# A hybrid decoder layer with a mixture of experts: another order of output projection and router, one ring slot and one early request more, another end of the last norm

## The chip, the cores and the metric

The kernel runs on one core of a Trainium2 chip. The metric is the device time of one execution in microseconds (us). A core has TensorE (PE) for matmuls, with its weight loads shown as PEld; VectorE (DVE); ScalarE (ACT); GpSimd (POOL); and SyncE (SP), whose queue issues most of the DMAs here. All engines take their instructions from queues of their own, in order, and wait for each other by semaphores. Matmul results land in the banks of PSUM, everything else lives in SBUF, and weights and inputs come from HBM.

## The reference

One layer over 512 tokens of width 1024. A first half mixes tokens; a second half is a feed-forward part with 32 experts, of which each token uses two.

```python
def hybrid_mixer(x, mem, ...):
    proj = x @ w_in                       # queries, keys, values, gates of three branches
    y_a = moba_attention(...); y_b = stick_breaking_attention(...); y_m = memory_attention(...)
    merged = (gates[:, :, 0] * (y_a @ w_br_moba) + gates[:, :, 1] * (y_b @ w_br_sb)
              + gates[:, :, 2] * (y_m @ w_br_mem))
    return merged @ w_out                 # the output projection

def hierarchical_moe(x, ...):
    g_p, g_idx = lax.top_k(softmax(x @ w_router_group + b_router_group), 1)
    e_logits = x @ w_router_expert + b_router_expert     # 4 groups of 8 experts
    top_l, top_i = lax.top_k(e_in_group, 2)              # two experts of the chosen group
    gate = g_p * softmax(top_l)
    ...                                                  # per expert e, on its tokens:
        h = silu(xb @ w_gate[e]) * (xb @ w_up[e]);  y = h @ w_down[e]
    ...                                                  # sum of gate * y over a token's experts

x = layer_norm(alpha * x + hybrid_mixer(x, mem, ...))
x = layer_norm(alpha * x + hierarchical_moe(x, ...))
```

All is float32. Each expert has 6 MB of weights, so 192 MB are read in one execution.

## The kernel before, in words

Tokens stand in four tiles of 128 (t = 0 to 3), channels in eight blocks of 128. Precision in the first half is kept by splitting each operand into a high and a low part of a shorter float and adding three products (mm3, L122): "woh" and "wol" are the parts of the output weights, "mgh" and "mgl" those of the merged branches.

**The end of the first half.** Attention and gates run as a list of jobs. The output projection of the first four channel blocks is done among them; of the last four blocks it is done behind them, in `project` (L825): for a tile t and a half of the columns (c = 0 or 1) nine matmuls for blocks 4 to 6 and three for block 7, whose merged branch is the last to be ready, into a bank of "dn". DVE adds the bank to x1 with row sums (L835), and `norm` follows for the tile: sums (L599), the square on ACT (L601), the second step (L602), two halves of subtract and scale (L606), a power on POOL (L603), two halves of scale and offset (L610). POOL then stores the tile to the scratch "xdr".

**The router**, per tile: T transposes x1 on PE and ACT copies it to "xt" (L648, L649); L multiplies it by the router's weights (L656), and DVE chooses group and experts from the logits in ten short operations (L661 to L672), the last of which writes "ab", the 0/1 table of the tile's experts; R counts places by small matmuls with "ab" (L679 to L682), and DVE turns the counts into places and these into the 0/1 matrix "sel" of the first pair of experts (L684 to L688, L732, L733); A gathers the tile's tokens of the first pair by matmuls with "sel" (L843). A pair is two experts with 64 places each. The string ORDER says in which order PE takes these steps: "G0" is `project` of tile 0, "G30" and "G31" the two halves of tile 3, "T0", "L0", "R0", "A0" the steps above. PE's order is fixed by it; the order of DVE, ACT, POOL and SP is made by a scheduler when the program is built, and is fixed too when it runs.

**The experts.** For each of 16 pairs: up and gate (`up`, L955, tile "gu"), the product (L964), a transpose ("ht"), down (L982, "dn"), and `combine`, which adds the result to x1 for all tiles by matmuls with the 0/1 matrix "sT" (L800, L801). Weights come in halves of 1 MB: two halves each of gate, up and down for two experts, 12 halves a pair, 192 in all. They land in a ring of RA + RB + RC + RD slots, 9 + 4 + 4 + 1 = 18, in four pools ("ring1" to "ring4"), and two halves more in a buffer "once", which is given up after its use. A slot is filled again when PE has used it. The pools open when their memory is free: ring2 before the projection, with 4 halves loaded early; ring1 when the branches are done; ring3 when the projection has read its weights; "once" and ring4 later in the router. `ahead(n)` asks for the next n halves on SP.

After pair 0 stands a loop (L1158) over experts with more than 64 tokens; with these inputs it runs zero times, but its count comes from a table that DVE makes during pair 0, and all engines meet in a barrier around it. Before it, `ahead(BEFORE)` with BEFORE = 6 asks for six halves; every later half is asked for behind the loop, when a slot comes free.

**The end.** `last_norm` scales and shifts x1 in 8 parts of 128 tokens by 512 columns: `inner` on DVE, then `outer`, which for the parts in BYDVE runs on DVE (L1079) and for the others as a matmul with a diagonal matrix onto a bank that holds the offset already (L1106, L1081), with a copy back by ACT (L1082). Each part is stored by SP in the order of the parts (`ship`, L1055).

Of the kernel before, what the change touches and what calls it, by code (L numbers as in the profile page):

```python
# [11 lines left out]
F32 = mybir.dt.float32  # L12
# [5 lines left out]
ALU = mybir.AluOpType  # L18
# [4 lines left out]
P = 128  # L23
# [10 lines left out]
WB, LOOK = 2, 1  # L34
F_M, F_A, F_B = 3.9, 3.9, 3.9
H = (slice(0, 64), slice(64, 128))
RA, RB, RC, RD = 9, 4, 4, 1
HALF = 2048
MIDP = 0
BEFORE = 6  # L40
CW = 184
BIG = 8192.0
XTB = 2
HTB = 1
BYDVE = ((3, 0), (3, 1))
BANKS = ("ht", "gu", "dn", "cb", "xgp", "cb", "", "")
FIRST = (2, 1)
ORDER = "G0 G1 T0 G2 L0 T1 G30 L1 R0 G31 A0 T2 L2 T3 R1 L3 R2 A1 R3 A2 A3"


@with_exitstack
def layer(ctx, tc, xT, xn, memT, w_qk, w_v, w_mk, w_mv, w_g, w_o, rb, oh, ln, wr, br,
# [69 lines left out]
    def mm3(o, pairs, start=True, stop=True):  # L122
        n = len(pairs)
        for i, (lh, ll, rh, rl) in enumerate(pairs):
            pe.matmul(o, lh, rh, start=start and i == 0, stop=False)  # L125
            pe.matmul(o, ll, rh, start=False, stop=False)  # L126
            pe.matmul(o, lh, rl, start=False, stop=stop and i == n - 1)  # L127
# [459 lines left out]
    def bank3(tag):  # L587
        return ps.tile([P, 512], F32, name=tag, tag=tag, bufs={"gu": 2, "dn": 2, "xgp": 1, "ht": 1, "cb": 2}[tag])
# [232 lines left out]
    pairs[0].start()  # L821
    first = []

    def project(t, cols=(0, 1)):

        ts = slice(t * P, (t + 1) * P)
        os_ = [bank3("dn") for c in cols]
        for ks in (range(3), range(3, 4)):
            for c, o in zip(cols, os_):
                r = slice(c * 512, (c + 1) * 512)  # L830
                mm3(o, [(mg[4 + k][0][:, ts], mg[4 + k][1][:, ts], wo[k][0][:, r], wo[k][1][:, r]) for k in ks],
                    start=ks[0] == 0, stop=ks[0] == 3)
        for c, o in zip(cols, os_):
            r = slice(c * 512, (c + 1) * 512)
            ve.scalar_tensor_tensor(out=x1[:, t, r], in0=x1[:, t, r], scalar=1.0, in1=o, op0=ALU.mult, op1=ALU.add,  # L835
                                    accum_out=sm[:, t, c:c + 1])
        if 1 in cols:
            norm(t, sm, lnb, op)
            gp.dma_start(xdr[ts, :], x1[:, t, :])
# [10 lines left out]
    with tc.manual_schedule(engines={mybir.EngineType.PE}):  # L850
        xt_ = {}
        for step in ORDER.split():
            t = int(step[1])
            if step[0] == "G":
                project(t, (0, 1) if len(step) == 2 else (int(step[2]),))
                if t == 0:
                    first += [bank3("xgp"), bank3("cb")]
            elif step[0] == "T":
                xt_[t] = turn_x(t)
            elif step[0] == "L":  # L860
                route(t, xt_[t])
            elif step[0] == "R":
                place(t)
            else:
                gather0(t)
        settle()
# [179 lines left out]
    def last_norm(gb):  # L1046

        col = lambda i: slice(i * 512, (i + 1) * 512)

        def inner(t, i):  # L1050
            x = x1[:, t, col(i)]
            ve.scalar_tensor_tensor(out=x, in0=x, scalar=sm2[:, t, 5:6], in1=gb[:, 0, col(i)], op0=ALU.add, op1=ALU.mult)  # L1052

        def ship(t, i):
            nc.sync.dma_start(out[t * P:(t + 1) * P, col(i)], x1[:, t, col(i)])  # L1055

        m, d = sm2[:, :, 5], sm2[:, :, 6]
        ve.tensor_tensor(out=m, in0=sm2[:, :, 0], in1=sm2[:, :, 1], op=ALU.add)
        ve.tensor_scalar(out=m, in0=m, scalar1=-1.0 / D, scalar2=None, op0=ALU.mult)
        ve.scalar_tensor_tensor(out=d, in0=sm2[:, :, 0], scalar=2.0 / D, in1=m, op0=ALU.mult, op1=ALU.add)  # L1060
        ve.tensor_tensor(out=d, in0=d, in1=d, op=ALU.mult)
        inner(0, 0)

        v = [sm2[:, :, i] for i in range(8)]
        ve.scalar_tensor_tensor(out=v[3], in0=v[3], scalar=EPS * D ** 3 / 4.0, in1=v[4], op0=ALU.add, op1=ALU.add)
        ve.scalar_tensor_tensor(out=v[3], in0=v[3], scalar=4.0 / D ** 3, in1=v[6], op0=ALU.mult, op1=ALU.subtract)
        gp.tensor_tensor(out=v[7], in0=v[3], in1=half.to_broadcast([P, TT]), op=ALU.pow)
        inner(0, 1)
        inner(1, 0)
        diag = late[0].tile([P, TT, P], F32, name="diag", tag="hT", bufs=1)  # L1070

        def spread(ts):
            ve.tensor_tensor(out=diag[:, ts, :], in0=ident.unsqueeze(1).to_broadcast([P, ts.stop - ts.start, P]),
                             in1=v[7][:, ts].unsqueeze(2).to_broadcast([P, ts.stop - ts.start, P]), op=ALU.mult)

        def outer(t, i):
            x = x1[:, t, col(i)]
            if (t, i) in BYDVE:
                ve.scalar_tensor_tensor(out=x, in0=x, scalar=v[7][:, t:t + 1], in1=gb[:, 1, col(i)], op0=ALU.mult, op1=ALU.add)  # L1079
            else:  # L1080
                pe.matmul(os_[t, i], diag[:, t, :], x, start=False, stop=True)  # L1081
                sc.copy(x, os_[t, i])  # L1082
            ship(t, i)

        inner(1, 1)
        spread(slice(0, 2))
        for t in range(2):
            outer(t, 0)
            outer(t, 1)
        inner(2, 0)  # L1090
        spread(slice(2, 4))
        outer(2, 0)
        inner(2, 1)
        outer(2, 1)
        inner(3, 0)
        inner(3, 1)
        outer(3, 0)
        outer(3, 1)

    os_ = {}  # L1100

# [6 lines left out]
    def last(hT):  # L1108
        pair = pairs[15]
        b = [None, None]  # L1110

        def part(c, ks):
            if ks[0] == 0:
                pair.room(c)
                b[c] = bank3("dn")
                held[:] = [weights(30 + q, 2, c) for q in range(2)]
            for k in ks:
                for q in range(2):
                    pe.matmul(b[c][H[q]], hT[:, k, H[q]], held[q][:, k * 512:(k + 1) * 512], start=k == 0, stop=k == 3)  # L1119

        part(0, range(4))
        pair.out = b[0]
        pair.finish(0)
        part(1, range(2))
        lnt = ring().rearrange("p (a b) -> p a b", b=D)
        for i in range(2):
            nc.sync.dma_start(lnt[:, i, :], ln[2 + i:3 + i, :].to_broadcast([P, D]))
        last_sums(0, ("cb", "xgp", "gu", "cb"))
        part(1, range(2, 4))
        ve.tensor_copy(pair.y_h[1], b[1])  # L1130
        ve.tensor_tensor(out=pair.y_l[1], in0=b[1], in1=pair.y_h[1].bitcast(F32), op=ALU.subtract)
        offset(lnt, 0, 2)
        last_sums(1, ("cb", "xgp", "gu", "cb"))
        offset(lnt, 2, 6)
        last_norm(lnt)

    hTs = []
# [20 lines left out]
    with tc.For_i(0, nov, 1) as i:  # L1158
# [13 lines left out]
        ve.tensor_copy(pair.si[0:64, 0:1], sp[0:64, 0:1])  # L1172
        ve.tensor_copy(pair.si[0:64, 2:3], sp[0:64, 1:2])
        pair.rows(64)
        pair.xg = late[0].tile([P, KT, 64], F32, name="xg_o")
        o = bank3("xgp")
        for k in range(KT):
            pe.transpose(o[:, k * 64:(k + 1) * 64], xrow[0][0:64, k * P:(k + 1) * P], ident[0:64, 0:64])
# [120 lines left out]
```

## Time and profile before

| | us |
|---|---|
| three runs | 942.25, 937.72, 940.51 (median 940.51) |
| the profiled execution | 942.12 |
| its span, first to last instruction | 940.3 |
| PE busy | 896.4 |
| DVE busy | 454.3 |
| ACT busy | 261.8 |

The span is the time from the first to the last instruction that the profiler recorded; the execution's own time has 1.8 us around it. Busy time alone doesn't say what sets the end: a matmul counts as busy while it is in the pipeline, and a program of several stages has another limit in each. The chain of waits names, from the last instruction back, what each step waited for. The windows give busy times, the granted share of PE's clock (PEclk: 1.00 is 2.4 GHz, 0.50 is 1.2 GHz), and the load of the 16 DMA engines in one stretch. A timeline lists instructions in order, like ones in one row.

### The profile page before, as it was taken

The page shows a single profiled execution, that of the slowest core. Times are in us where ns is not written, and L with a number is a line of the kernel's source. Part 1 is how long each engine was busy: PE and PEld are TensorE (multiplying, and loading weights), DVE is VectorE, ACT ScalarE, POOL GpSimd, SP SyncE. Part 2 cuts the span into 40 slices and gives each one's busy share as a digit, 9 for nine tenths or more (in the row PEclk, how much of TensorE's full clock was granted, in tenths as well). Part 3 has the DMA queues.
Part 4 walks back from the last instruction along what each step waited for, and adds up shares of the span by engine and source line. Part 5 has one row for each costly group of instructions (what it writes and reads, how often), then busy time and mean ns, then how long its engine had stood idle before and what let it go on. Part 6 is the DMA issues. An engine that isn't in the chain of part 4 may idle for free. (4 is left out here: it accounts for less than half of the span.)

```text
span 940.3 us, 11698 instructions
## 1 busy us (share of the span) xinstructions
PE 896.4 (95%) x4444; PEld 554.5 (59%) x4444; DVE 454.3 (48%) x1050; ACT 261.8 (28%) x498; POOL 42.5 (5%) x40
## 2 busy tenths in 40 slices
PE   6999999999999999999989999999999999999996
PEld 6788888777688888878624444344443334334433
DVE  5776776665764553277454324243332234212226
ACT  6465564554422223323311111011110011001104
POOL 2000000000000000042000000000000000000000
PEclk9999999999999999999999999999999999999999
DMA  8233241221344432289869999999999999999982
GB/s 290 93 112 114 70 144 68 68 68 68 135 183 143 184 108 90 90 319 365 329 248 410 422 421 419 420 419 421 419 421 420 419 420 420 421 421 420 420 363 90
DMA packets 46946, 255.58 MB, mean 272 GB/s; under 512 B 6958, under 2 KB 8149, under 8 KB 22440
## 3 DMA queue, kind: packets, MB, share of 16 engines
q1 hardware_dynamic: 42480, 247.84, 66.7%
q0 software_dynamic: 2736, 6.11, 1.7%
q10 hardware_dynamic: 1672, 0.85, 0.3%
q8 instruction: 36, 0.59, 0.3%
q14 instruction: 22, 0.18, 0.1%
HBM read 254.43 MB, written 4.20 MB: 275 GB/s over the span
## 5 line engine op out<-in xcount | busy, mean ns | idle before, releaser
L955 PE MATMUL gu<-r,xg 128*64 128x512 f32 x1008 | 238.5, 599 | 13.4 <-DMA r<-in_we_dram 12.6
L955 PEld LDWEIGHTS gu<-r,xg 128*64 128x64 f32 x1008 | 78.6, 137 | 160.6 <-issue 131.6
L104 DVE TENSOR_TENSOR wl<-wraw,wh 128x1024 fp32r<-128x1024 f32 (+2 forms) x71 | 81.0, 1144 | 88.6 <-ACT wh L103 88.5
L125 PE MATMUL pj<-xh,wh 128*128 128x512 f32 x304 | 120.6, 397 | 0.0
L126 PE MATMUL pj<-xh,wl 128*128 128x512 f32 x304 | 118.6, 390 | 1.1 <-DVE wl L104 1.1
L127 PE MATMUL pj<-xl,wh 128*128 128x512 f32 x304 | 118.7, 391 | 0.0
L982 PE MATMUL dn<-r,hT 128*64 128x512 f32 x480 | 109.4, 598 | 5.4 <-ACT hT L972 5.4
L103 ACT CAST wh<-wraw 128x1024 fp32r<-128x1024 f32 (+2 forms) x71 | 70.3, 990 | 80.5 <-PE z L127 23.4
L803 DVE TENSOR_TENSOR x<-x,cb 128x512 f32<-128x512 f32 x60 | 38.4, 681 | 110.2 <-PE cb L801 110.2
L982 PEld LDWEIGHTS dn<-r,hT 128*64 128x64 f32 x480 | 31.9, 136 | 61.4 <-issue 52.1
L125 PEld LDWEIGHTS pj<-xh,wh 128*128 128x128 f32 x304 | 57.0, 188 | 14.4 <-issue 2.1
L126 PEld LDWEIGHTS pj<-xh,wl 128*128 128x128 f32 x304 | 57.1, 188 | 12.8 <-DVE wl L104 1.4
L127 PEld LDWEIGHTS pj<-xl,wh 128*128 128x128 f32 x304 | 57.1, 188 | 12.1
L964 DVE SCALAR_TENSOR_TENSOR u<-gu,si,g 128x512 f32<-128x512 f32 x16 | 12.0, 751 | 101.8 <-PE gu L955 96.7
L766 ACT COPY xg<-xgp 128x512 f32<-128x512 f32 x15 | 8.8, 587 | 160.5 <-PE xgp L765 160.5
L103 ACT CAST y_h<-dn 128x512 fp32r<-128x512 f32 x31 | 18.2, 586 | 100.8 <-PE dn L982 97.0
L963 ACT ACTIVATE g<-gu 128x512 f32<-128x512 f32 x16 | 9.6, 599 | 123.0 <-PE gu L955 123.0
L386 ACT ACTIVATE gt<-pj 128x512 f32<-128x512 f32 x24 | 14.4, 598 | 89.9 <-PE pj L127 89.9
L803 DVE TENSOR_TENSOR x<-x,dn 128x512 f32<-128x512 f32 x60 | 38.3, 679 | 0.0
L104 DVE TENSOR_TENSOR y_l<-dn,y_h 128x512 fp32r<-128x512 f32 x31 | 21.3, 688 | 33.0 <-ACT y_h L103 32.9
L755 POOL DMA_INDIRECT xrow<-xdr,ix x15 | 14.9, 994 | 398.9 <-DVE sel L732 316.3
L800 PE MATMUL cb<-y_h,sT 128*128 128x512 f32 x64 | 28.7, 448 | 0.0
(636 smaller groups left out, 1310.3 us busy)
## 6 DMA issues: line engine op xcount, KB each, us to landing
r<-in_we_dram SPq DMA_DIRECT2D x189, 1024.0 KB, 20.2
wraw<-in_w_g_dram SPq DMA_DIRECT2D x32, 512.0 KB, 3.3
wraw<-in_w_qk_dram SPq DMA_DIRECT2D x14, 512.0 KB, 3.3
wraw<-in_w_v_dram SPq DMA_DIRECT2D x16, 384.0 KB, 3.3
wraw<-in_w_o_dram SPq DMA_DIRECT2D x8, 512.0 KB, 3.3
xraw<-in_xT_dram SPq DMA_DIRECT2D x4, 512.0 KB, 7.9
x<-in_xn_dram SPq DMA_DIRECT2D x4, 512.0 KB, 5.6
xdr<-x POOLq DMA_DIRECT2D x4, 512.0 KB, 8.6
```

The source lines that it names most:

```text
L103: sc.copy(dst_h, src)
L104: (gp if eng is gp else ve).tensor_tensor(out=dst_l, in0=src, in1=dst_h.bitcast(F32), op=ALU.subtract)
L125: pe.matmul(o, lh, rh, start=start and i == 0, stop=False)
L126: pe.matmul(o, ll, rh, start=False, stop=False)
L127: pe.matmul(o, lh, rl, start=False, stop=stop and i == n - 1)
L386: after(sc.activation(out=t, in_=o, func=AF.Sigmoid), last_exp[0])
L755: gp.indirect_dma_start(xrow[0][0:n], None, xdr, bass.IndirectOffsetOnAxis(ap=ix[0:n, 0:1], axis=0), bounds_check=S - 1, oob_is_err=False)
L800: pe.matmul(o, sT, self.y_h[c][0:n], start=True, stop=False)
L803: ve.tensor_tensor(out=x1[:, t, r], in0=x1[:, t, r], in1=o, op=ALU.add)
L955: pe.matmul(o[H[q]], pairs[p].xg[:, k, H[q]], held[q][:, k % 4 * 512:k % 4 * 512 + 512], start=k == 0, stop=k == KT - 1)
L964: ve.scalar_tensor_tensor(out=hs, in0=u, scalar=pairs[p].si[:, 0:1], in1=gs, op0=ALU.mult, op1=ALU.mult)
L982: pe.matmul(o[H[q]], hT[:, k, H[q]], w[q][:, k * 512:(k + 1) * 512], start=k == 0, stop=k == 3)
```

## The change

- **Order of the steps.** A step P does the nine matmuls of blocks 4 to 6 of a tile for both column halves, a step Q the three of block 7 and what follows them. The new order has P and Q for tiles 0 to 2 and G30, G31 for tile 3, then the router's steps in another sequence. Tile 1's banks are "ht" and "cb", so that P0 and P1 can both be open. The banks of the gather ("xgp", "cb") are taken at tile 3 instead of tile 0.
- **Ring.** RC is 5 instead of 4: 19 slots. Memory for it comes from a tile inside the loop that now shares a buffer.
- **Requests before the loop.** BEFORE is 7 instead of 6.
- **The last norm.** Part (2, 1) joins (3, 0) and (3, 1) on VectorE; five parts instead of six run on PE and ACT. All parts are stored in the order SHIP, behind the computation.

```diff
-RA, RB, RC, RD = 9, 4, 4, 1
+RA, RB, RC, RD = 9, 4, 5, 1
...
-BEFORE = 6
+BEFORE = 7
...
-BYDVE = ((3, 0), (3, 1))
-BANKS = ("ht", "gu", "dn", "cb", "xgp", "cb", "", "")
+SHIP = ((0, 0), (0, 1), (2, 1), (1, 0), (3, 0), (1, 1), (3, 1), (2, 0))
+BYDVE = ((2, 1), (3, 0), (3, 1))
+BANKS = ("ht", "gu", "dn", "cb", "xgp")
...
-ORDER = "G0 G1 T0 G2 L0 T1 G30 L1 R0 G31 A0 T2 L2 T3 R1 L3 R2 A1 R3 A2 A3"
+ORDER = "P0 P1 Q0 P2 Q1 T0 Q2 G30 L0 T1 G31 L1 R0 A0 T2 R1 A1 L2 T3 R2 A2 L3 R3 A3"
...
-    def project(t, cols=(0, 1)):
+    parts = {}
+
+    def project(t, cols=(0, 1), ks=range(4)):
...
-        os_ = [bank3("dn") for c in cols]
-        for ks in (range(3), range(3, 4)):
-            for c, o in zip(cols, os_):
+        for c in cols:
+            if (t, c) not in parts:
+                parts[t, c] = bank3(("ht", "cb")[c] if t == 1 else "dn")
+        for kk in (range(3), range(3, 4)):
+            for c in cols:
                 r = slice(c * 512, (c + 1) * 512)
...
+        if 3 not in ks:
+            return
...
-                if t == 0:
+                if t == 3 and len(first) == 0:
                     first += [bank3("xgp"), bank3("cb")]
+            elif step[0] in "PQ":
+                project(t, ks=range(3) if step[0] == "P" else range(3, 4))
...
-        inner(2, 1)
-        outer(2, 1)
-        inner(3, 0)
-        inner(3, 1)
-        outer(3, 0)
-        outer(3, 1)
+        for t, i in ((2, 1), (3, 0), (3, 1)):
+            inner(t, i)
+            outer(t, i)
+        for t, i in SHIP:
+            ship(t, i)
...
-        offset(lnt, 2, 6)
+        offset(lnt, 2, 5)
...
-        pair.xg = late[0].tile([P, KT, 64], F32, name="xg_o")
+        pair.xg = late[0].tile([P, KT, 64], F32, name="xg_o", tag="sq", bufs=1)
```

What the build makes of it is seen best on two engines. On PE, in the router behind the projection, before the change, from A0 on (xgp and cb from "sel" are A, gu from ident is T, cb from "wrt" is L, the ht rows are R):

```order
L843 MATMUL xgp<-sel,x_2546 128x128 x4
L843 MATMUL cb<-sel,x_2546 128x128 x4
L648 MATMUL gu<-ident,x_2546 128x128 x8
L656 MATMUL cb<-wrt,xt 128x40 x8
L648 MATMUL gu<-ident,x_2546 128x128 x8
L679 LDWEIGHTS oneb
L679 MATMUL ht<-e64b,oneb 128x32
L681 LDWEIGHTS oneb
L681 MATMUL ht<-ab,oneb 128x32
L682 LDWEIGHTS trib
L682 MATMUL ht<-ab,trib 128x32
L656 MATMUL cb<-wrt,xt 128x40 x8
```

and with the change, from A0 on:

```order
L851 MATMUL xgp<-sel,x_2546 128x128 x4
L851 MATMUL cb<-sel,x_2546 128x128 x4
L649 MATMUL gu<-ident,x_2546 128x128 x8
L680 LDWEIGHTS oneb
L680 MATMUL ht<-e64b,oneb 128x32
L682 LDWEIGHTS oneb
L682 MATMUL ht<-ab,oneb 128x32
L683 LDWEIGHTS trib
L683 MATMUL ht<-ab,trib 128x32
L851 MATMUL xgp<-sel,x_2546 128x128 x4
L851 MATMUL cb<-sel,x_2546 128x128 x4
L657 MATMUL cb<-wrt,xt 128x40 x8
```

R1 and A1 stood behind T2, L2 and T3; now they follow T2, A1 comes right behind R1, and L2 behind A1. Line numbers are one higher with the change, and eight to ten higher from `project` on.

On DVE, before the change, the stretch that ends with tile 0's "sel" (L732 and L733 write "sel" from the places in "dst"; L684 to L688 are tile 0's places, L661 to L668 belong to tile 1's route):

```order
L835 SCALAR_TENSOR_TENSOR x_2546,sm<-x_2546,dn 128x512
L661 TENSOR_TENSOR rw<-cb,brt 128x40
L684 TENSOR_TENSOR rw<-ht,cs 128x32
L663 MAX rw<-rw 128x8
L685 SCALAR_TENSOR_TENSOR rw<-rw,ht 128x32
L664 MAX_INDEX ix<-rw 128x8
L688 SCALAR_TENSOR_TENSOR junk,dst<-oh_3754,rw 128x32
L665 TENSOR_SCALAR rw<-cs,ix 128x4
L688 SCALAR_TENSOR_TENSOR junk,dst<-oh_3754,rw 128x32
L732 TENSOR_SCALAR sel<-cs,dst 128x128
L666 TENSOR_TENSOR rw<-rw 128x32
L733 SCALAR_TENSOR_TENSOR sel<-cs,dst,sel 128x128
```

and with the change, the stretch that ends with the same "sel" (now L733, L734; L603 to L611 are the norm of tile 3):

```order
L689 SCALAR_TENSOR_TENSOR junk,dst<-oh_3754,rw 128x32
L669 MAX rw<-rw 128x8
L603 TENSOR_SCALAR sm<-sm 128x1
L607 SCALAR_TENSOR_TENSOR x_2546<-x_2546,sm,lnb 128x512 x2
L611 SCALAR_TENSOR_TENSOR x_2546<-x_2546,sm,lnb 128x512 x2
L670 MAX_INDEX ix<-rw 128x8
L689 SCALAR_TENSOR_TENSOR junk,dst<-oh_3754,rw 128x32
L733 TENSOR_SCALAR sel<-cs,dst 128x128
L671 TENSOR_SCALAR oh_3754<-cs,ix 128x32
L673 TENSOR_SCALAR oh_3754<-cs,ix 128x32
L672 SCALAR_TENSOR_TENSOR ab<-cs,ix,oh_3754 128x32
L734 SCALAR_TENSOR_TENSOR sel<-cs,dst,sel 128x128
```

The second step and the four halves of tile 3's norm, which stood behind this "sel", now stand ahead of it, and so does the end of tile 1's route.

## Rows read from the trace of the kernel before

**Rows 1.** The chain of waits in order of time; columns: start us, us, what.
```profile
586.82 20.62 DMA r<-in_we_dram
...
874.35 20.59 DMA r<-in_we_dram
```

**Rows 2.** Busy us by window: length, PE, PEld, DVE, ACT, POOL; PEclk, DMA share, GB/s.
```profile
413.20:416.60 3.40, 3.40 (x10) 2.58 (x9) 1.66 (x6) 0.75 (x1) 0.00 (x0) 0.50 1.01 426
443.90:450.70 6.80, 6.72 (x38) 6.55 (x37) 4.68 (x39) 1.08 (x2) 0.00 (x0) 0.50 0.99 373
456.00:475.00 19.00, 17.61 (x92) 7.14 (x94) 5.78 (x39) 3.46 (x5) 1.09 (x1) 1.00 0.93 359
480.00:485.00 5.00, 2.92 (x18) 1.00 (x16) 1.07 (x4) 0.59 (x1) 0.00 (x0) 0.99 0.00 0
600.00:880.00 280.00, 266.02 (x1210) 111.87 (x1207) 89.84 (x217) 30.61 (x55) 8.87 (x9) 1.00 1.01 420
```

**Rows 3.** Timeline of SP: start us, us issuing, engine line op out<-in xcount.
```profile
437.54 0.81 SPq L534 DMA_DIRECT2D r<-in_we_dram  x2
...
484.54 2.10 SPq L534 DMA_DIRECT2D r<-in_we_dram  x4
...
599.71 279.93 SPq L534 DMA_DIRECT2D r<-in_we_dram  x110
...
936.02 0.91 SPq L1055 DMA_DIRECT2D out_dram<-x  x2
```

**Rows 4.** Waits of SP: who waited for whom, us in total, times, longest.
```profile
SPq L1158 <- DVEq L1157: 4.4, 1, 4.4
```

**Rows 5.** Timeline of PE around the router; in brackets idle time before, ended by whom.
```profile
406.39 0.39 PE L125 MATMUL dn<-woh,mgh 128*128 128x512 f32 x1
...
410.27 0.39 PE L127 MATMUL dn<-wol,mgh 128*128 128x512 f32 x1
411.99 0.49 PE L125 MATMUL dn<-woh,mgh 128*128 128x512 f32 x1 [1.33 <-ACT mgh L103]
...
421.02 1.03 PE L648 MATMUL gu<-ident,x 128*128 128x128 f32 x8
...
427.38 1.87 PE L656 MATMUL cb<-wrt,xt 128*128 128x40 f32 x16
...
437.35 1.06 PE L843 MATMUL xgp<-sel,x 128*128 128x128 f32 x8
...
441.30 1.98 PE L656 MATMUL cb<-wrt,xt 128*128 128x40 f32 x16 [1.13 <-ACT xt L649]
...
455.94 7.09 PE L955 MATMUL gu<-r,xg 128*64 128x512 f32 x32 [0.77 <-ACT xg L869]
...
474.16 3.65 PE L982 MATMUL dn<-r,hT 128*64 128x512 f32 x16 [0.68 <-ACT hT L972]
```

**Rows 6.** Timeline of DVE around the router.
```profile
429.29 0.20 DVE L661 TENSOR_TENSOR rw<-cb,brt 128x40 f32<-128x40 f32 x1 [1.02 <-PE cb L656]
...
431.18 0.23 DVE L672 TENSOR_SCALAR oh<-cs,ix 128x32 f32<-128x32 f32 x1
...
438.28 0.21 DVE L599 TENSOR_SCALAR sm<-sm 128x1 f32<-128x1 f32 x1
...
439.93 1.41 DVE L606 SCALAR_TENSOR_TENSOR x<-x,sm,lnb 128x512 f32<-128x512 f32 x2
...
451.52 0.19 DVE L684 TENSOR_TENSOR rw<-ht,cs 128x32 f32<-128x32 f32 x1 [0.72 <-PE ht L682]
...
452.72 0.34 DVE L733 SCALAR_TENSOR_TENSOR sel<-cs,dst,sel 128x128 f32<-128x128 f32 x1
```

**Rows 7.** Timelines of DVE and ACT at the end of the program.
```profile
932.38 1.41 DVE L1079 SCALAR_TENSOR_TENSOR x<-x,sm,r 128x512 f32<-128x512 f32 x2
...
934.98 0.59 ACT L1082 COPY x<-cb 128x512 f32<-128x512 f32 x1 [0.27 <-PE cb L1081]
```

**Rows 8.** Landing of the loads into r (the halves), all of the program.
```profile
DMA to landing us min/median/max: 5.1/20.2/22.6
```

More of the change, by code (lines that the diff above doesn't have):

```diff
@@ L822, in layer @@
     first = []
-    def project(t, cols=(0, 1)):
+    parts = {}
+    def project(t, cols=(0, 1), ks=range(4)):
         ts = slice(t * P, (t + 1) * P)
-        os_ = [bank3("dn") for c in cols]
-        for ks in (range(3), range(3, 4)):
-            for c, o in zip(cols, os_):
-                r = slice(c * 512, (c + 1) * 512)
-                mm3(o, [(mg[4 + k][0][:, ts], mg[4 + k][1][:, ts], wo[k][0][:, r], wo[k][1][:, r]) for k in ks],
-                    start=ks[0] == 0, stop=ks[0] == 3)
-        for c, o in zip(cols, os_):
+        for c in cols:
[3 more added lines that the diff above has]
+            for c in cols:
+                r = slice(c * 512, (c + 1) * 512)
+                if kk[0] in ks:
+                    mm3(parts[t, c], [(mg[4 + k][0][:, ts], mg[4 + k][1][:, ts], wo[k][0][:, r], wo[k][1][:, r]) for k in kk],
+                        start=kk[0] == 0, stop=kk[0] == 3)
+        if 3 not in ks:
+            return
+        for c in cols:
             r = slice(c * 512, (c + 1) * 512)
-            ve.scalar_tensor_tensor(out=x1[:, t, r], in0=x1[:, t, r], scalar=1.0, in1=o, op0=ALU.mult, op1=ALU.add,
+            ve.scalar_tensor_tensor(out=x1[:, t, r], in0=x1[:, t, r], scalar=1.0, in1=parts[t, c], op0=ALU.mult, op1=ALU.add,
                                     accum_out=sm[:, t, c:c + 1])
@@ L1082, in outer @@
                 sc.copy(x, os_[t, i])
-            ship(t, i)
         inner(1, 1)
```

## The prediction, made before the changed kernel was run

> **What bounds the kernel now.** I read the chain of waits first, then the busy time by window, then the queue of SP (which issues every weight load), and last the timelines of PE and DVE around the router.
>
> The chain says that from 586.8 us to 894.9 us PE waits for expert weights: 15 links of some 20.5 us, each "DMA r<-in_we_dram" [rows 1]. The windows show why: from 600 to 880 us the DMA engines are busy all the time (share 1.01, 420 GB/s), while between 480 and 485 us they move nothing [rows 2]. So the end is set by one stream: 192 halves of expert weights (1 MB each), and the time is the moment at which this stream begins to run without holes, plus the halves still missing then, plus the tail. In the steady stretch SP issues 110 halves from 599.71 us within 279.9 us [rows 3]: 279.6 / 109 = 2.57 us a half, the xrow gathers included.
>
> The moment at which it begins to run is the end of the barrier around the overflow loop. SP waits there for DVE, 4.4 us at the last [rows 4], and issues the next four halves at 484.54 us [rows 3]. Counted in the code, 26 halves are asked for before it: 4 early, 9 in ring1, 2 in "once", 4 in ring3, 1 in ring4, 6 ahead of the loop. All have landed when the loop ends (nothing moves in 480 to 485 us), so what ring3, ring4 or the early loads gain or lose before that has no weight in itself. Two things have: when the loop ends, and how many halves have landed by then. The loop's end hangs on PE: its first expert matmul starts at 455.94 us [rows 5], the loop ends 28.6 us later, and nothing between the two is changed but one DMA.
>
> **The two halves more.** RC = 5 puts one more slot in the ring and BEFORE = 7 one more request ahead of the loop: 28 halves instead of 26 at the loop's end, 2 x 2.57 = 5.1 us less stream behind it. After the loop three slots instead of four are free at once; the requests that follow are paced by PE, and each comes one request later in the count, which I price at 0.4 us. The seventh request has to wait for its slot, the first one of the down projection: PE's matmuls on it run from 474.16 us for 3.65 us [rows 5], so SP issues it near 477.6 us. Queued behind it on SP are only the load of the loop's count and the barrier, which opens shortly before 484.54 us. A lone half lands 5.1 us after its issue [rows 8], at 482.7 us, while SP still waits for DVE. Cost nothing; up to 2.6 us if it ended last. The Trainium skill (DMA: Bandwidth & Descriptors, section Bandwidth) gives 6.15 us for a DMA of 1 MB; by that the half would land at 483.8 us, in the last microsecond before the barrier opens, and the sum would be up to 0.5 us more. This case's row says 5.1 us, and the row decides.
>
> **The order of projection and router.** First what it gives. PE no longer stands still for the last branch (1.33 us before, at 411.99 us), because P0 and P1 (36 matmuls) come in front of the first that needs it. Eighteen matmuls take 406.39 to 410.5 us, 0.228 us each [rows 5]. Up to the end of G31 the new order has all 96 of them (21.9 us), two T (0.8 us each: the row's 1.03 less the overlap with the next matmul) and one L (1.7 us): 25.2 us, plus two waits of 0.3 us for a bank of "dn" that DVE has not read yet: 432.2 us. Before, SP sees that end at 437.54 us [rows 3]. The projection ends 5 us earlier, and ring3 loads earlier; as said, this alone buys nothing.
>
> Now what it costs. DVE's queue stands in program order, and in the new one the last operation of tile 0's selection (sel) stands behind the norm of tile 3. Step by step: L1 ends at 434.0; the sums of tile 3 wait behind the first operation of tile 1's route, so the norm's first step comes at 434.4 (before: 438.28 us). From that step to its second, over ACT's square, 1.6 us, then 2.8 us for the four halves of which two are the row of 1.41 us, with POOL's power beside them [rows 6]: 438.8. Seven short operations, 1.1 us: sel is ready at 440.0. A0 on PE starts there, against 437.35 us before [rows 5], and PE has waited 6 us in two pieces.
>
> Behind A0 the old order has 15.9 us of mixed work in which each chain of DVE is covered by another step of PE. The new order is T2 R1 A1 L2 T3 R2 A2 L3 R3 A3, in which it isn't. From R to sel DVE takes 452.72 + 0.34 - 451.52 = 1.5 us; from the logits to ab 2.1 us and the last operation, 2.3 to 2.5 us [rows 6]. So: A0 1.8 (twice the row of 1.06 [rows 5] less overlaps) to 441.8; T2 to 442.6; R1, wait 1.5, A1 to 446.0; L2 to 447.9; ab 2.3 us, of which T3 covers 0.8, R2 at 450.2; wait 1.5, A2 to 453.6; L3 to 455.4; ab 2.3, R3 at 457.8; wait 1.5, A3 from 459.5 to 461.3. The copy of the first half of xg lies beside the second half of A3. The experts would start at 461.3, 5.4 us later than before, if PE ran at 2.4 GHz throughout.
>
> It will not. Behind its short stops before, 1.33 us at 411.99 us and 1.13 us at 441.30 us [rows 5], the granted clock is 0.50 (1.2 GHz) in 413.2 to 416.6 and in 443.9 to 450.7 us [rows 2]: 6.8 of the 18.6 us from A0 to the experts. The new order stops PE twice before A0 and five times behind it, for 1.5 to 2.5 us each. Its work from A0 on is 4 x 1.8 + 2 x 0.8 + 2 x 1.7 + 0.4 = 12.6 us at full clock. Bounds: nothing lost (5.4 us later), or all of it at the lower level, at most doubled (18 us later). I take 5 us, 0.4 of it, a little over the share that the old stretch has in the row: the experts start 10.5 us later, and so does the loop's end. The Trainium skill (TensorE: Matmul & The Clock Gate, section What's actually happening) states that the lower clock is the default and that activity releases it. By that rule the stretch could stay low until the experts run densely, which is the rival of 954 us below; the old trace has the clock back at 450.7 us, before the experts, so I give it little.
>
> **The tail.** One copy on ACT and its matmul less: the last copy, from 934.98 us for 0.59, goes, 0.86 us by PE's step; DVE's last pair at 932.38 us [rows 7] becomes later by one operation of 0.7 us and ends near 934.6, beside ACT's new last copy at 934.7. Before, two stores of 0.45 us were queued behind the last copy (936.02 us, 0.91 us for both [rows 3]); with SHIP there is one, the last copy's own. Together 0.9 + 0.9, less what DVE's end takes away: 1.5 us less. Bounds 0 and 1.8.
>
> **The sum.** The profiled execution took 942.1 us (its span of 940.3 and 1.8 around it): + 10.5 (experts later) - 5.1 (two halves) + 0.4 - 1.5 = 946.4 us. It is 1.6 us above the median of the runs, 940.51; on the median the sum would be 944.8. I predict 945.8, between them and nearer the sum.
>
> **The rivals.**
> 1. The clock holds: the waits are there, at 2.4 GHz. 5.4 instead of 10.5: 941.3 us. For it: a stop of 0.77 us just before the experts [rows 5] is followed by a clock of 1.00 from 456 to 475 us [rows 2]. Against: both dips listed.
> 2. The clock stays low from A0 on: 18 instead of 10.5, 953.9 us.
> 3. The other side: the new order does what it says. If the experts start no later than before (the waits on DVE covered by what I have not seen, such as a norm of tile 3 that is done earlier by as much as G31 is), the two halves and the tail are left: 942.1 - 5.1 + 0.4 - 1.5 = 935.9 us, faster. It decides as soon as the experts start less than 1.5 us later. For it: PE's stall for the last branch goes, and G31 ends 5 us earlier. Against: the order of DVE's queue, and that A3 is alone at the end.
> 4. The seventh half doesn't come in time, or the barrier waits for it: one half gained, or a loop longer by up to 2.6 us: 949.0 us. For it: its slot is free only 6 us before the barrier opens. Against: 5.1 us suffices.
>
> **How the numbers follow.** Forecast 0.52, rivals 1 to 4: 0.18, 0.08, 0.12, 0.10. The forecast's own range is 943 to 949.5 (clock loss 1.5 to 8 us). The range of 8 in 10 reaches down through rival 1 and leaves most of 3 and 2 outside: 938.5 to 950.5. A difference of 0.5% is 4.7 us, about what the runs can tell from none: slower is above 945.2, which takes two thirds of the forecast and nearly all of rivals 2 and 4: 0.52. Within 0.5%: a third of the forecast, rival 1: 0.36. Faster: rival 3, 0.12.
>
> **What would show it.** In the changed kernel's trace: no wait for mgh in G0; the first ring3 load behind G31 near 432; A0's first matmul near 440 with an idle time that DVE's sel ended; four waits of 1.5 us before A1, A2, A3 and of over 1.5 before R2 and R3; a granted clock of 0.50 in several stretches from 437 to 466; the first expert matmul between 461 and 470; loop end 28.6 us behind it; DMA idle for over 10 us before it; then 164 halves at 2.57. It is wrong if the experts start before 457, if the loop's end does not follow their start, or if the stream has holes behind it.

## The result, and the profile after

| | before | with the change |
|---|---|---|
| median of the runs beside each other | 940.25 (4 runs, 937.72 to 942.25) | 951.81 (4 runs, 950.21 to 954.17) |
| a second time | 940.92 (11 runs) | 951.59 (6 runs, 948.11 to 953.5) |
| the profiled execution, its span | 942.12, 940.3 | 950.21, 948.4 |

The change makes the kernel slower: ratio 1.0126 [1.0091, 1.0162], the second time 1.0111 [1.0087, 1.0134]. Predicted were 945.8 us and a range up to 950.5: the direction is right, the size is not. The two profiled executions are 8.1 us apart, the medians 11.6: before's profile is nearly as slow as its slowest run here (942.25), the profile after is the fastest of its four. Why runs of one kernel differ is read further down.

The end is still set by one stream of halves. In the chain of waits after, as in [rows 1], PE waits for expert weights through links of some 20 us, now from 699 us on instead of 587; between the loop's end and there the chain is PE's own work. Columns: start us, us, what.

```profile
695.73 3.47 PE gu L965 x15
699.19 20.46 DMA r<-in_we_dram
...
883.24 19.79 DMA r<-in_we_dram
```

PE after, in the router, against [rows 5] (start us, us, engine line operation; in brackets the idle time before, and what ended it):

```profile
432.38 0.40 PE L128 MATMUL dn<-wol,mgh 128*128 128x512 f32 x1
...
435.53 0.18 PE L683 MATMUL ht<-ab,trib 128*128 128x32 bf16 x1 [1.02 <-DVE ab L672]
440.49 2.07 PE L851 MATMUL xgp<-sel,x 128*128 128x128 f32 x8 [4.79 <-DVE sel L734]
...
447.16 1.16 PE L851 MATMUL xgp<-sel,x 128*128 128x128 f32 x8 [1.56 <-DVE sel L734]
...
453.29 0.18 PE L683 MATMUL ht<-ab,trib 128*128 128x32 bf16 x1 [1.40 <-DVE ab L672]
455.03 1.97 PE L851 MATMUL xgp<-sel,x 128*128 128x128 f32 x8 [1.56 <-DVE sel L734]
...
462.78 0.18 PE L683 MATMUL ht<-ab,trib 128*128 128x32 bf16 x1 [2.27 <-DVE ab L672]
464.60 2.08 PE L851 MATMUL xgp<-sel,x 128*128 128x128 f32 x8 [1.63 <-DVE sel L734]
...
468.32 2.17 PE L965 MATMUL gu<-r,xg 128*64 128x512 f32 x8
```

G31 ends at 432.8 (before 437.5), but A0 starts at 440.49 (before 437.35) and the experts at 468.32 (before 455.94): 12.4 us later. The waits of PE between 430 and 470 us, grouped (who waited for whom, us in total, times, longest), are all for DVE:

```profile
PE xgp L851 <- DVE sel L734: 9.5, 4, 4.8
PE ht L683 <- DVE ab L672: 4.7, 3, 2.3
```

DVE after, ahead of A0, against [rows 6]: the norm's second step and its four halves (L603, L607, L611), and behind them the "sel" that A0 waits for.

```profile
436.47 0.13 DVE L603 TENSOR_SCALAR sm<-sm 128x1 f32<-128x1 f32 x1
436.52 1.41 DVE L607 SCALAR_TENSOR_TENSOR x<-x,sm,lnb 128x512 f32<-128x512 f32 x2
437.84 1.41 DVE L611 SCALAR_TENSOR_TENSOR x<-x,sm,lnb 128x512 f32<-128x512 f32 x2
...
440.09 0.35 DVE L734 SCALAR_TENSOR_TENSOR sel<-cs,dst,sel 128x128 f32<-128x128 f32 x1
```

The windows after, against [rows 2] (length, then busy us of PE, PEld, DVE, ACT, POOL; PEclk, DMA share, GB/s): in three of them PE's granted clock is 0.50 to 0.53, and behind the loop, from 497.10 on, the DMA engines move 392 GB/s in the first 50 us, where they move 420 later.

```profile
440.00:445.00 5.00, 4.51 (x21) 4.51 (x22) 0.44 (x3) 0.69 (x1) 0.12 (x1) 0.51 1.00 422
445.00:455.00 10.00, 5.50 (x52) 5.12 (x50) 4.69 (x28) 3.46 (x6) 0.00 (x0) 1.00 0.85 356
455.00:458.50 3.50, 3.47 (x17) 3.48 (x17) 0.00 (x0) 0.00 (x0) 0.00 (x0) 0.53 0.00 0
462.00:468.50 6.50, 4.08 (x19) 3.67 (x20) 4.92 (x28) 2.17 (x4) 0.00 (x0) 0.50 0.18 33
497.10:547.10 50.00, 49.32 (x238) 20.87 (x240) 20.79 (x57) 5.50 (x10) 1.99 (x2) 1.00 0.98 392
600.00:880.00 280.00, 268.02 (x1228) 110.12 (x1226) 91.61 (x228) 31.79 (x57) 9.84 (x10) 1.00 1.01 420
```

Three stages cover the whole difference of the two profiled executions; the first matmul of the projection starts at 406.4 us in both. The loop ends at 497.12 instead of 484.49: 12.6 later (predicted 10.5). From there to DVE's last sum of the residual (the moment at which all weights are used) it takes 436.5 us instead of 440.6: 4.2 less (predicted 5.1 - 0.4 = 4.7). From that sum to the end of the span 14.8 instead of 15.2: 0.4 less (predicted 1.5). Together 8.1.

### The profile page after: what moved, and what is told of

It reads as the page before. It is cut to its first block, busy times and chain, and to the rows that moved or that the text cites. A ratio compares the mean times of both kernels' runs of the same rounds, so it can differ in the third digit from the quotient of the medians.

```text
span 948.4 us, 11686 instructions
## 1 busy us (share of the span) xinstructions
PE 894.7 (94%) x4440; PEld 553.5 (58%) x4440; DVE 456.5 (48%) x1051; ACT 261.2 (28%) x497; POOL 43.1 (5%) x40
## 5 line engine op out<-in xcount | busy, mean ns | idle before, releaser
L126 PEld LDWEIGHTS pj<-xh,wh 128*128 128x128 f32 x304 | 57.0, 188 | 14.3 <-issue 2.1
L105 DVE TENSOR_TENSOR y_l<-dn,y_h 128x512 fp32r<-128x512 f32 x31 | 21.3, 689 | 32.9 <-ACT y_h L104 32.9
```

Of the source, the lines that this page charges most:

```text
L105: (gp if eng is gp else ve).tensor_tensor(out=dst_l, in0=src, in1=dst_h.bitcast(F32), op=ALU.subtract)
```

## The experiments

In the table: median and number of runs; ratio to the kernel before on the same chip, with its 95% interval; then from the one profile of each kernel the start of A0, the time from A0 to the first expert matmul, how much of that time had a granted clock of 0.50, the halves asked for when the loop ends, and the time from the loop's end to the last sum.

| kernel | median (n) | ratio | A0 | A0 to experts | low clock in it | halves | loop to last sum |
|---|---|---|---|---|---|---|---|
| before | 939.96 to 940.92 | | 437.35 | 18.6 | 6.8 | 26 | 440.6 |
| changed | 951.81 (4) | 1.0126 [1.0091, 1.0162] | 440.49 | 27.8 | 14.1 | 28 | 436.5 |
| changed again | 951.59 (6) | 1.0111 [1.0087, 1.0134] | 442.00 | 29.1 | 18.8 | 28 | 436.5 |
| e1 order only | 954.77 (5) | 1.016 [1.014, 1.018] | 442.62 | 27.8 | 14.1 | 26 | 439.8 |
| e2 all but the order | 936.63 (12) | 0.9965 [0.9952, 0.9979] | 435.32 | 15.7 | 0 | 28 | 436.7 |
| e3 slot and request | 936.37 (12) | 0.9962 [0.9944, 0.998] | 436.17 | 20.0 | 10.2 | 28 | 437.0 |
| e4 last norm only | 940.81 (12) | 1.0013 [0.9994, 1.0033] | 436.79 | 15.7 | 0 | 26 | 441.3 |
| e5 new up to A0 | 942.34 (12) | 1.0023 [1.0009, 1.0038] | 441.21 | 17.2 | 2.9 | 28 | 437.4 |
| e6 new from A0 on | 950.39 (6) | 1.0111 [1.0083, 1.014] | 437.48 | 30.8 | 19.4 | 28 | 436.7 |
| e7 old router, P and Q | 935.40 (12) | 0.9949 [0.993, 0.9968] | 435.33 | 15.7 | 0 | 28 | 437.4 |
| e8 waits filled | 946.32 (6) | 1.0067 [1.0044, 1.009] | 440.17 | 22.4 | 0 | 28 | 438.6 |
| e9 e7, waits filled | 936.26 (6) | 0.9952 [0.9935, 0.9969] | 437.54 | 15.2 | 0 | 28 | 437.1 |
| e11 e7, six requests | 935.05 (6) | 0.9947 [0.9928, 0.9967] | 434.81 | 15.7 | 0 | 27 | 437.9 |
| e12 changed, six requests | 951.27 (6) | 1.0125 [1.0098, 1.0153] | 439.91 | 28.0 | 14.3 | 27 | 437.4 |
| e13 slot only | 937.85 (12) | 0.997 [0.9946, 0.9994] | 437.47 | 19.9 | 10.2 | 27 | 439.1 |
| e14 request only | 939.24 (12) | 0.9991 [0.9971, 1.0012] | 437.08 | 18.5 | 6.8 | 27 | 439.5 |

The last five columns come from one execution each, and kernels that agree in what a column depends on show how far it scatters: A0 between 434.8 and 437.5 with the old steps ahead of it, the last column at 440.6 and 441.3 for 26 halves in the old order, and between 436.5 and 438.6 for 28 halves.

**The parts, one by one (e1 to e4).** Edits: on the changed kernel, ring and last norm put back (e1); on the kernel before, all but ORDER and `project` (e2), only these two lines and the shared buffer (e3), only SHIP, BYDVE, BANKS and what uses them (e4).

```diff
 e3
-RA, RB, RC, RD = 9, 4, 4, 1
+RA, RB, RC, RD = 9, 4, 5, 1
-BEFORE = 6
+BEFORE = 7
```

> Only the new order of projection and router; ring, requests ahead of the loop and last norm as before. Theory (the order alone makes the kernel slower, because the experts start later and the one stream behind them is as long as before): first expert matmul 10 to 16 us later than the 455.94 of before, the loop's end by as much, and the whole kernel by the same: 950 to 956 us, ratio to before 1.011 to 1.017. Rival (the order costs little, and what costs is the seventh request, which holds SP or the barrier): 940 to 945 us.

> Everything of the change but the order: 19 slots, seven requests, the new last norm; projection and router as before. Theory: experts start at 456 as before, two halves fewer behind the loop, 430.3 us from its end to the last landing become 425.8: 4.5 us less, and the new last norm gives 0 to 1.5: 934 to 936 us, ratio 0.993 to 0.996. Rival (the seventh request or the new ring costs): 940 us or more.

> Only the ring of 19 slots and seven requests ahead of the loop. Theory: 4.5 us less, 935 to 936.5 us; 28 halves landed when the loop ends, which is no later than the 484.5 of before. Rival (the seventh half holds the barrier): loop's end 2 to 3 us later and the time 938 us or more.

> Only the new last norm (three parts on DVE, five on PE and ACT, stores in the new order behind the computation). By the prediction's term 1.5 us less: about 938.5 us. By the pair of profiles nothing: from the last landed half to the end of the span 25.5 us in both, so 940 us, since what the shorter chain on PE and ACT gives is taken back by DVE and by the stores behind it.

The order costs by itself 14.0 us between the medians, and everything else together makes the kernel faster. The rival (the seventh request holds SP or the barrier) falls: with the request and without the order the loop ends 28.6 us behind the experts' start, as before. The last norm is worth 0.0 between the medians, at best 0.06%. In the profiles the stretch from the last sum to the end takes 15.2 us with the old last norm (before, e1, e13) and 14.8 with the new one (changed and again, e4, e6, e11) where PE's granted clock holds until its last matmul; with an earlier part at 0.50, 16.8 and 16.9 (e3, e14) and 15.6 to 16.6 (e2, e5, e7, e8, e9, e12). So the new last norm gives 0.35 us in the profiles, and a fall of the clock there goes with up to 1.8. e2 came out 0.6 above its range. The sum of the parts, 14.0 - 4.4 + 0.0 = 9.6, is a little under the 11.6 and 10.7 that were measured; the intervals of e1 and e3, 1.9 and 1.7 us either way, cover the difference.

**Where in the order (e5, e6, e7).** All three are the changed kernel with another ORDER:

```diff
-ORDER = "P0 P1 Q0 P2 Q1 T0 Q2 G30 L0 T1 G31 L1 R0 A0 T2 R1 A1 L2 T3 R2 A2 L3 R3 A3"
 e5
+ORDER = "P0 P1 Q0 P2 Q1 T0 Q2 G30 L0 T1 G31 L1 R0 A0 T2 L2 T3 R1 L3 R2 A1 R3 A2 A3"
 e6
+ORDER = "P0 P1 Q0 P2 Q1 T0 Q2 L0 T1 G30 L1 R0 G31 A0 T2 R1 A1 L2 T3 R2 A2 L3 R3 A3"
 e7
+ORDER = "P0 P1 Q0 P2 Q1 T0 Q2 L0 T1 G30 L1 R0 G31 A0 T2 L2 T3 R1 L3 R2 A1 R3 A2 A3"
```

> The changed kernel with the new sequence up to A0 (so tile 0's sel stands behind tile 3's norm) and the old one from A0 on (T2 L2 T3 R1 L3 R2 A1 R3 A2 A3). Theory (the serial chain behind A0 is most of the loss, the late A0 a smaller part): A0 at 440.5 as in the changed kernel, then 15.7 to 18.6 us to the experts as the profiles with the old sequence show: experts at 456 to 459 against 468.3, 9 to 12 us less than the changed kernel: 940 to 943 us. Rival (the late A0, with PE's long stop before it, is most of the loss): 947 us or more.

> The changed kernel with P and Q, but the old sequence up to A0 (R0 ahead of G31, so sel is ready when G31 ends), and the new sequence from A0 on. Theory: A0 at about 436, then the 27.8 us of the changed kernel from A0 to the experts: 463.8, 4.5 us earlier than the changed kernel: 945 to 949 us. Rival (late A0 is most of the loss): 942 us or less.

> The changed kernel with P and Q for tiles 0 to 2 and the old sequence of the router throughout: PE's stop for the last branch (1.33 us) is covered, nothing else of the old order is lost; 19 slots, seven requests, new last norm. Theory: A0 at about 436, experts at 451.5 to 454.5, 1.3 us earlier than without P and Q: 934 to 936.5 us, ratio to before 0.993 to 0.996, the fastest of all. Rival (P and Q themselves cost, by the banks of tile 1 or later sums): 938 us or more.

The medians of e5 and e7 lie in their ranges. Against e7, which shares P and Q and the chip with both, the late A0 alone (e5) costs 6.9 us and the new sequence behind A0 alone (e6) 15.0; both together cost 16. They don't add, and e6 came out above what was expected. Its PE and its DVE show why; first PE (columns as above):

```profile
437.48 1.06 PE L851 MATMUL xgp<-sel,x 128*128 128x128 f32 x8
...
444.24 1.16 PE L851 MATMUL xgp<-sel,x 128*128 128x128 f32 x8 [3.86 <-DVE sel L734]
```

and DVE in the same stretch of e6:

```profile
440.07 1.41 DVE L607 SCALAR_TENSOR_TENSOR x<-x,sm,lnb 128x512 f32<-128x512 f32 x2
441.39 1.41 DVE L611 SCALAR_TENSOR_TENSOR x<-x,sm,lnb 128x512 f32<-128x512 f32 x2
...
443.83 0.35 DVE L734 SCALAR_TENSOR_TENSOR sel<-cs,dst,sel 128x128 f32<-128x128 f32 x1
```

A0 is ahead of the changed kernel's by 3.0 us, but now the norm of tile 3 stands ahead of tile 1's "sel", and A1 waits for it 3.86 us instead of 1.56; more of the way is at 0.50, too (19.4 us against 14.1). The norm has to pass DVE somewhere; in these kernels it costs PE no wait only beside steps of PE that don't hang on DVE. The old sequence has them there (T2, L2, T3 behind A0); the new one has R1 and A1. In e7, which keeps that cover, A0 comes at 435.33 and the experts 15.7 us behind it:

```profile
435.33 1.06 PE L851 MATMUL xgp<-sel,x 128*128 128x128 f32 x8
...
450.99 7.09 PE L965 MATMUL gu<-r,xg 128*64 128x512 f32 x32
```

e7 is one of the two fastest kernels here (the other is e11). What P and Q themselves give can't be seen in the medians: the intervals of e7 and of e2, which has the old order without them, overlap. The traces say why. From the first matmul of the projection to A0 it takes 29.27 us in e7 and in e11, and 29.76 in e2: 0.5 us less. P and Q cover the stop for the last branch (1.32 us in e2, and 0.22 behind it), but PE now stops in front of T1, 1.18 us:

```profile
426.78 1.33 PE L649 MATMUL gu<-ident,x 128*128 128x128 f32 x8 [1.18 <-issue]
```

The profile names no releaser for this stop. T1 reads tile 1's norm, and DVE starts the last two halves of it (L611) at 425.93 us, against 423.26 in e2 without such a stop; so the later norm of tile 1 is the likely cause, which no run tests.

**The clock (e8, e9).** A new step F puts n matmuls on PE whose result nobody reads; ORDER of e8 is that of the change with F in front of the waits.

```diff
+            elif step[0] == "F":
+                if not fill:
+                    fill.append(bank3("dn"))
+                for _ in range(t):
+                    pe.matmul(fill[0][:, 0:256], ident, x1[:, 0, 0:256], start=True, stop=True)
 e8
+ORDER = "... G31 L1 F2 R0 F10 A0 T2 R1 F3 A1 L2 T3 F3 R2 F3 A2 L3 F5 R3 F3 A3"
 e9 (on e7)
+ORDER = "... G31 A0 T2 F2 L2 T3 R1 L3 R2 F1 A1 F1 R3 A2 A3"
```

> The changed kernel with 29 matmuls (128x256, f32, some 0.43 us each) that nobody reads, put on PE where it waits: 2 before R0, 10 before A0, 3 before A1, A2, A3 and R2, 5 before R3. The chains on DVE stay as they are. Theory (of the 27.8 us from A0 to the experts some 5 are the low clock behind the waits, the rest is waits and work): the granted clock stays 1.00, 22.5 to 23.5 us from A0 to the experts, who start near 463.5, 5 us earlier than in the changed kernel: 945 to 948 us. Rival (the clock falls for another reason, or PE's speed is not what these steps hang on): the dips or the 27.8 us stay, 951 to 954 us.

> The kernel of the covered order with P and Q (19 slots, seven requests, new last norm) and four matmuls (128x256, f32) that nobody reads, put where PE still stops: two before L2, one before A1, one before R3. Theory (the spread of the kernel before, 936.5 to 945.1 in 29 runs, is the low clock behind the short stops of the router, there in some executions and not in others): the clock holds in every execution, experts 15.7 us behind A0, no run above 937, median 934 to 935. Rival (the spread has another cause, or the low clock comes from the stretch ahead of A0): spread and median as without them, 933.7 to 938.9, median 935.4.

In e8 the window from A0 to the experts (columns as in the windows above) has the full clock:

```profile
440.00:462.50 22.50, 21.53 (x158) 19.21 (x158) 10.37 (x64) 8.69 (x11) 0.00 (x0) 1.00 0.58 244
```

A0 stays where it was (440.17), the chains on DVE are the same, and the experts start 22.4 us behind it instead of 27.8. The kernel takes 946.3 us, 5.3 less than the changed one. So of the 16 us between the changed kernel and e7 (951.6 against 935.4), some 5.3 are the low clock around the waits, and the rest are the waits: A0 4.8 us later than in e7, and 22.4 us instead of 15.7 behind it. This agrees with what the Trainium skill says (TensorE: Matmul & The Clock Gate, section What's actually happening), that activity is what releases the lower clock; here even work without a use keeps it released.

The same clock accounts for much of what the profiles of one order differ by. With the old sequence the experts start 15.7 us behind A0 where the clock holds (e2, e4, e7, e11), 18.5 and 18.6 with 6.8 us at 0.50, 19.9 and 20.0 with 10.2 us: the same instructions there each time. It falls in two more places: ahead of A0, where the way from the first matmul of the projection takes 29.8 us (e2, e3, e13) or, with a part at 0.50 behind the stop for the last branch, 31.0 to 31.2 (before, e4, e14); and behind the last sum, as said above. That the spread of the runs comes from it is likely, but only one execution of each kernel shows its stretches. In e9 no run is above 937 and the spread is 1.7 us in 6 runs, against 5.2 in 12 of e7 (4.1 in 6 of e11, without fillers). But its median is not better (936.26 against 935.40), against the expectation, and its one profile has the clock at 0.50 from 428.3 us, ahead of A0, and again behind the last sum: the fillers gain nothing that can be seen where the stops are short, and the clock does not hold everywhere.

**The changed kernel again (e10).** No edit.

> The changed kernel once more, with a second profile. Theory (the order costs 14.0 by itself, the two halves give 4.4, the last norm 0): 950 us, 9.6 above before, ratio 1.010; the experts start 27.5 to 28.5 us behind A0, with some 10 us of it at the low clock. Rival (something in the three parts adds up worse than by itself): 952 us or more.

951.59, 10.7 above before on that chip where the parts add up to 9.6, and near the rival's 952. The difference is inside the intervals of the parts, so neither is excluded. What slot and request do is the next point.

**Slot and request (e11 to e14).** e11 and e12 are e7 and the changed kernel with one line back; e13 and e14 are the kernel before with one line of the two in e3 each.

```diff
 e11, e12
-BEFORE = 7
+BEFORE = 6
```

> The kernel of the covered order with P and Q, 19 slots, new last norm, and six requests ahead of the loop instead of seven. Theory (the seventh half lands ahead of the loop's end and is worth one half of the stream): 27 halves when the loop ends, 2.57 us later than with seven: about 938 us. Rival (the seventh request gains nothing, since its data come when the stream runs anyway, or it holds the barrier): 935.4 us or less.

> The changed kernel with six requests ahead of the loop instead of seven; 19 slots, new order, new last norm. Theory (behind the loop a request goes out when PE frees the slot 19 halves back, whatever was asked for ahead of the loop; so the seventh request only moves one half into time in which the DMA engines stand idle, and holes in the stream behind the loop take it back): 951 to 952.5 us, as with seven; 27 halves at the loop's end, and the stream behind it without the holes that the changed kernel has. Rival (each half asked for ahead of the loop is one less behind it, as the prediction counted): 2.57 us more, 954 us.

> Only the fifth slot of ring3, on the kernel before: 19 slots, six requests, old order, old last norm. Theory (the slot is what gives: every request behind the loop goes out one slot earlier): 936 to 938 us, most of the 4.4 us that slot and request gave together. Rival (slot and request give 2.57 each less the pacing): 938.5 us.

> Only the seventh request, on the kernel before: 18 slots, seven requests, old order, old last norm. Theory (it gives nothing without the slot; three requests instead of two have to wait for PE behind the loop, and the stream has more holes): 940 to 942 us, ratio to before 0.999 to 1.002. Rival (one half less behind the loop): 938 us, ratio 0.997.

The seventh request gives nothing that can be seen in the medians: 951.27 without it and 951.6 with it in the new order, 935.05 and 935.40 in e11 and e7, and alone on the kernel before 0.9991 [0.9971, 1.0012]. The fifth slot alone gives 0.997 [0.9946, 0.9994]. The first 50 us behind the loop's end show where the request's half goes. e12, with six requests (columns as in the windows above):

```profile
496.70:546.70 50.00, 49.19 (x238) 20.77 (x240) 20.78 (x57) 5.50 (x10) 2.00 (x2) 1.00 0.99 405
```

The changed kernel, with seven, moves 392 GB/s in the same 50 us. On the kernel before it is 400 GB/s with six requests:

```profile
484.50:534.50 50.00, 49.36 (x230) 20.77 (x232) 20.76 (x57) 5.50 (x10) 1.99 (x2) 0.97 0.98 400
```

and 386 with the seventh added (e14):

```profile
484.10:534.10 50.00, 49.16 (x230) 20.71 (x232) 20.77 (x57) 5.49 (x10) 1.99 (x2) 0.97 0.96 386
```

(405 - 392) / 420 x 50 = 1.5 us of the stream are lost to holes, and (400 - 386) / 420 x 50 = 1.7. The reason stands in SP's queue. The 32nd half is asked for at 493.64 us on the kernel before, at 493.29 with the seventh request (e14) and at 491.79 with the fifth slot (e13). One row each in this order; columns: start us, us issuing.

```profile
493.64 0.33 SPq L534 DMA_DIRECT2D r<-in_we_dram  x1
```

```profile
493.29 0.33 SPq L534 DMA_DIRECT2D r<-in_we_dram  x1
```

```profile
491.79 0.33 SPq L534 DMA_DIRECT2D r<-in_we_dram  x1
```

Behind the loop's end (484.49, 484.11 and 485.90 us) that is 9.15, 9.18 and 5.89 us. The seventh request leaves every later request where it was: behind the loop a half is asked for when PE has freed a slot. The DMA engines have one half less to move there, and run dry until PE catches up. One slot more brings each request to where the one ahead of it stood (the 31st goes out 5.70 us behind the loop's end on the kernel before). From the loop's end to the last sum the seventh request gives 0.9 us (e12 and the changed kernel), 0.5 (e11 and e7), 1.1 (before and e14) and 2.1 (e13 and e3); the slot 2.5 (e1 and e12), 1.6 (before and e13) and 2.5 (e14 and e3). Such a difference of two executions is uncertain by 0.7 or more (before and e4: 440.6 and 441.3 with nothing changed there), so neither figure is sharp, though the slot gives more than the request at each place where both were tried. Its own price in holes is small: 395 GB/s in the first 50 us in e13 against 400 before, 405 in both e1 and e12.

## Why the prediction missed, step by step

All three terms of the sum came out to the slow side. The largest miss is the order's: "the experts start 10.5 us later" was 12.4 in the profiles, and the order cost 14.0 in the medians.

**What bounds the kernel** held: the end is the loop's end plus a stream plus a tail, and the loop ends 28.5 to 29.1 us behind the experts' start in all of these profiles. What the prediction left out is the stretch before 586.8 us, where it began to read the chain: from the loop's end to there, and to 699 us after, the chain is PE's own work, and PE sets when requests go out.

**The order.** Nearly all of its mechanism is in the trace. No wait for mgh in G0; G31 ends at 432.8 (432.2 predicted), the first ring3 load is at 432.81; A0 at 440.49 (440.0), its idle time ended by DVE's "sel"; 1.56, 1.56 and 1.63 us before A1, A2, A3 (1.5); 1.40 and 2.27 before R2 and R3; the clock at 0.50 in three stretches between 438 and 469; the experts inside the interval named. From A0 to the experts at full clock 22.4 us (e8) instead of 21.3; the clock's loss 5.4 instead of 5. Against the profile of before this makes 12.4 where "the experts start 10.5 us later" stood. But the term was set against one execution that had lost 18.6 - 15.7 = 2.9 us to the low clock behind A0, and 30.95 - 29.76 = 1.2 us ahead of it. Against runs as they fall, the order costs 14.0 (e1), 3.5 more than the step said.

**The two halves.** The step that failed in its mechanism: "28 halves instead of 26 at the loop's end, 2 x 2.57 = 5.1 us less stream behind it", with 0.4 for the pacing. 28 halves were there, the seventh was asked for in time (SP stood at the barrier for 3.8 us behind it; in e14 it landed at 482.66 us, 5.2 us after its issue, with the loop's end at 484.11) and none of its cost fell on the loop, as predicted. But the stream behind the loop has holes that take 1.5 of the seventh half's 2.57 us back: the pacing that was priced at 0.4. In the new order slot and request together give 439.8 - 436.5 = 3.3 us (e1 against the changed kernel; 3.2 between the medians) instead of 4.7; in the old order 3.6 (before and e3) and 4.6 (e4 and e2), 4.4 between the medians (e3). So the count of landed halves was wrong as a mechanism, and near in size.

**The tail.** 1.5 was predicted, 0.4 is in the profiles, 0.0 between the medians (e4). The copy that goes saves what the step said: ACT's last copy ends 9.6 us behind the last sum instead of 10.4. The rest was wrong. The last operations of DVE and ACT after, against [rows 7]:

```profile
942.53 0.75 DVE L1089 SCALAR_TENSOR_TENSOR x<-x,sm,r 128x512 f32<-128x512 f32 x1
```

```profile
942.58 0.59 ACT L1092 COPY x<-xgp 128x512 f32<-128x512 f32 x1 [0.27 <-PE xgp L1091]
```

DVE, with one part more, ends 0.1 us after ACT, and SHIP puts its store ahead of ACT's last one, so the last result comes 0.75 us earlier behind the last sum. Behind that result SP issues three stores before and two after, where the step had left one, and the two take longer than the three; SP's timeline before, then after:

```profile
935.59 1.33 SPq L1055 DMA_DIRECT2D out_dram<-x  x3
```

```profile
943.31 1.54 SPq L1065 DMA_DIRECT2D out_dram<-x  x2
```

**The sum.** On the pair of profiles: the loop's end 12.6 later instead of 10.5, the halves with their pacing 4.2 instead of 4.7, the tail 0.4 instead of 1.5. That is 2.1 + 0.5 + 1.1 = 3.7 on the 946.4 of the sum, 950.1 where 950.21 was measured. The forecast took 0.6 off towards the median of before, and the profile after is the fastest of its four, 1.6 under their median. The parts measured by themselves (14.0 - 4.4 + 0.0) put the change at 949.9 on the 940.25 of before, inside the range; the 1.9 that are left to 951.81, and 1.1 the second time, aren't explained by a run here and lie within the intervals. No single term decided: all three were off in the same direction, and the range, which let each err by itself, ended 1.3 us short. The rival with a clock that stays low (953.9) was nearest in number, but isn't what happened: 445 to 455 us ran at 1.00.

## What to carry to other kernels

Before a step is put earlier on one engine, look at what the waited-for engine has queued ahead of its answer: work of 4.4 us (the norm, from its first step to its last half) cost no wait beside matmuls that don't need that engine (e7), and elsewhere it only moved from one wait to the next: 4.8 us before A0 in the changed kernel, 3.86 instead of 1.56 before A1 in e6. A prefetch is worth its bytes only if the slots behind it are not the limit: ask when the next requests can go out, not only how much has landed. And where one profiled execution contains a loss that comes and goes, price a change against runs without it too.

## What was not expected of the hardware

How much the short stops cost in clock: with stops of 1.4 to 2.3 us behind A0, and the steps of the router between them, 14 to 19 of the 28 to 31 us to the experts had a granted clock of 0.50 in the new order, a different part in each execution. The clock may also couple PE with the stream, which no run shows by itself: behind the loop, with the same 26 halves, the kernel before (clock 0.97 over the 50 us, with a stretch at 0.50 just behind the loop) moves 400 GB/s in the first 50 us, e1 (1.00 throughout) 405, and the time to the last sum is 440.6 against 439.8. The difference is small, and no run takes that clock alone away.
